# Attention units pipelined in a fixed TensorE order among projection steps, and x's last transposes one block later

## The chip, the cores and the metric

One core of a Trainium2 chip runs the whole program in one launch. The metric is the device time of one execution in microseconds (us), median of three executions. The engines: PE (TensorE: matrix products and transposes), ACT (ScalarE), DVE (VectorE), POOL (GpSimd) and SP (which issues DMAs). Each works its own queue in the order in which its instructions were placed, and waits at an instruction until its inputs are ready and its output buffer is free.

## What is computed

Four layers of a decoder trunk, of kinds S5, HGRN2, attention, S5, on 512 tokens of width 1024. Each is `h = h + rms_norm(branch(rms_norm(h)))`. The attention layer (layer 2), cut to what matters:

```python
proj = h @ w_in                       # q 1024, k 256, v 256, z 1024
q, k = rope(q + b), rope(k + b)       # 16 query heads, 4 key heads of 64
scores = q . k / 8                    # blocks of 128 queries, this and the block before, masked
p = softmax over (scores, sink)       # the sink is one learnt logit per head
o = p @ v
out = (o * silu(z)) @ w_out
```

## The kernel before, in words

**Products.** All projections are done with three products of split numbers: hi x hi, hi x lo, lo x hi. Weights come in chunks of 256 features. ACT makes each chunk's high part (`whi`, L112), DVE its low part (`wlo`, L113). x is transposed by PE (tile `xtp`, L206), and ACT and DVE copy it out as `xh` and `xl` (L210, L211). A block of 128 features over all tokens takes 24 products `pj` 512 wide (`ws`, L146).

**Order.** A scheduler places the instructions inside each engine's queue. Its priorities follow the order in which the program is written, its choice a cost model of its own.

**First blocks of a layer** (`first_blocks`, L214): the first four blocks of features are worked in two halves of the tokens, 24 products 256 wide for each block and half. The first two blocks' first halves run first. Then the tokens' blocks 2 and 3 are transposed (`norm_xt`, L193): before the third and the fourth block's first half. In the attention layer the four blocks are k (two) and chunk 0 of q (two).

**Attention** (`layer_at`, L960). The rest of the projection is q chunks 1 to 3, v, and z chunks 0 to 3. After k and each q chunk comes `at_rope` (L875): ACT copies the products out (`rraw`, L880), four DMAs issued by ACT swap halves of the partitions (`rsw`, L884), DVE and POOL multiply by cosine and sine (L885, L886), DVE adds (L887). `rraw` and `rsw` have one buffer each.

The attention itself is `at_core(p, n)` (L889) for pair p of key heads and query block n, and each call has two units b2, so 16 units in all. A unit: four score products `scps`, two for either key head of the pair; one head lies in the upper 64 rows of PE's array, the other in the lower ("row halves"). DVE adds the mask and takes the maximum (L916), then `nm` (L920); ACT takes four exps with their sums (L925) and one more for the sink (`es`, L929); DVE adds, inverts and scales (L930, L932, L936); PE transposes the result (`ptp`, L940), ACT copies it out (`pt`, L941). After the second unit the product with v is taken (`aops`, L945) and ACT copies it over q (L949). For n = 0 scores are 128 wide, otherwise 256. A sigmoid and a multiplication for each block of z (L1013, L1014), and `at_gate` (L951) multiplies by z and splits.

PSUM banks go by tags: `ca` 2 (scores and `xtp`), `cb` 1 (`ptp`), `cc` 1 (`aops`), `pj` 4. The order in which cores, chunks of q and z, and gates are written is the table `ATSEQ` (L47): `c00 q2 c01 q3 c02 c03 z0 c10 z1 c11 ...`, and `plan_weights` (L56) loads weights in the same order.

Of the kernel before, what the change touches and what calls it, by code (L numbers as in the profile page):

```python
# [16 lines left out]
P = 128  # L17
# [28 lines left out]

ATSEQ = "c00 q2 c01 q3 c02 c03 z0 c10 z1 c11 g00 g01 z2 g02 g03 c12 z3 c13 g10 g11 g12 g13".split()  # L47


class Trunk:  # L50
# [4 lines left out]
    def plan_weights(self):  # L55
        seq = []  # L56
        for L in self.layers:
            kind, j = L % 3, L // 3
            if kind == 0:
                seq += [("s5_in", j, c) for c in range(8)]  # L60
                seq += [("s5_glu", j, c) for c in range(4)]
                o = "s5_out"
            elif kind == 1:
                for p in range(4):
                    seq += [("hg_in", j, c) for c in (p, 4 + p, 8 + p, 12 + p)]
                o = "hg_out"
            else:
                seq += [("at_in", j, c) for c in (4, 0, 5, 1) + tuple(int(t[1]) + 6 * (t[0] == "z") for t in ATSEQ if t[0] in "qz")]
# [71 lines left out]
    def ws(self, ps, w, fb, x, n0, n1):  # L140
# [73 lines left out]
    def first_blocks(self, L, evacs):  # L214
# [3 lines left out]
        for half in range(2):  # L218
            for b in range(4):
                if half == 0 and b >= 2:  # L220
                    for _ in self.norm_xt(L, (b,)):
                        pass
                self.ws(pss[b][:, half * 256:half * 256 + 256], w[b // 2], b % 2, self.x, half * 256, half * 256 + 256)
        for b in range(4):
# [664 lines left out]
    def at_core(self, p, n):  # L889

        nc, s = self.nc, self.scr
        lo = 0 if n else 128
        qs = slice(n * 128, n * 128 + 128)
        ks = slice(max(0, n - 1) * 128, n * 128 + 128)
        wd = 256 - lo
# [3 lines left out]
        ops = self.psum.tile([P, 4, 128], F32, tag="cc", name="aops", bufs=1)  # L899
        pts = [s.tile([P, 2, 4, 128], F32, tag=f"pt{i}", name="pt", bufs=1) for i in range(2)]  # L900
        f0 = lo // 128
        for b2 in range(2):
            bs = slice(2 * b2, 2 * b2 + 2)
            pss, sms = [], []
            for i in range(2):
                r = slice(64 * i, 64 * i + 64)
                ps = self.psum.tile([P, 2, 256], F32, tag="ca", name="scps", bufs=2)
                for bb in range(2):
                    nc.tensor.matmul(ps[:, bb, lo:256], lhsT=self.q[r, 4 * p + 2 * b2 + bb, qs], rhs=self.k[r, p, ks], start=True, stop=True)  # L909
                pss.append(ps)  # L910
            for i in range(2):
                sm = s.tile([P, 2, 256], F32, tag="sm", name="sm", bufs=3)
# [20 lines left out]
            for i in range(2):  # L933
                sm = sms[i]
                for bb in range(2):
                    nc.vector.tensor_scalar(out=sm[:, bb, lo:256], in0=sm[:, bb, lo:256], scalar1=rd[:, i, bb:bb + 1], scalar2=None, op0=ALU.mult)  # L936
# [4 lines left out]
                nc.scalar.activation(out=pts[i][:, f0:2, bs, :], in_=tp[:, f0:2], func=AF.Copy)  # L941
        for f in range(f0, 2):
            for i in range(2):
                kv = 2 * p + i
                nc.tensor.matmul(  # L945
                    ops[64 * i:64 * i + 64].rearrange("p b q -> p (b q)"), lhsT=self.v[:, n - 1 + f, kv * 64:kv * 64 + 64],
                    rhs=pts[i][:, f].rearrange("p b q -> p (b q)"), start=f == f0, stop=f == 1)

        nc.scalar.activation(out=self.q[:, 4 * p:4 * p + 4, qs], in_=ops, func=AF.Copy)  # L949
# [10 lines left out]
    def layer_at(self, L, nxt):  # L960
# [6 lines left out]
        with self.scratch():  # L967
# [21 lines left out]
            def qch(c):  # L989
                w = self.w_next("at_in")  # L990
                pss = []
                for fb in range(2):
                    ps = self.pj()
                    self.ws(ps, w, fb, self.x, 0, T)
                    pss.append(ps)
                self.at_rope(pss, bq[:, 2 * c:2 * c + 2], self.q[:, 2 * c:2 * c + 2, :])

            bv = s.tile([P, 2, T], F32, tag="misc", name="bv", bufs=1)[:, 0, 0:256]
# [7 lines left out]
            qch(1)  # L1006
            def zch(c):
                w = self.w_next("at_in")
                for fb in range(2):
                    ps = self.pj()  # L1010
                    self.ws(ps, w, fb, self.x, 0, T)
                    zz = self.z[:, 2 * c + fb, :]
                    nc.scalar.activation(out=zz, in_=ps, func=AF.Sigmoid)  # L1013
                    nc.vector.tensor_tensor(out=zz, in0=ps, in1=zz, op=ALU.mult)  # L1014

            for step in ATSEQ:
                if step[0] == "c":
                    self.at_core(int(step[1]), int(step[2]))
                elif step[0] == "g":
                    self.at_gate(int(step[1]), int(step[2]))  # L1020
                elif step[0] == "q":
                    qch(int(step[1]))
                else:
                    zch(int(step[1]))
# [185 lines left out]
```

## Time and profile before

| | us |
|---|---|
| median of 3 runs | 1125.99 |
| lowest, highest | 1124.99, 1126.99 |
| the profiled execution | 1127.56 |
| its span in the trace | 1125.8 |
| PE busy | 1039.3 (92%) |
| DVE busy | 783.4 (70%) |
| ACT busy | 516.8 (46%) |
| POOL busy | 233.2 (21%) |

The profiled execution is one of its own, 1.57 above the median; its span begins at the first instruction that the trace shows. The mean granted clock of PE was 0.968 of full speed. In the trace the first blocks of layers 1, 2 and 3 lie at 290 to 319, 604 to 633 and 839 to 869, the attention units, with what is left of the projection among them, at 671.5 to 806. Busy times of engines overlap, so their shares don't add up.

### The profile page before, as it was taken

To read this page: it belongs to the slowest core of one execution; us is meant where nothing else is said; L and a number is where in the kernel's file an instruction comes from. 1 tells how busy PE (TensorE), PEld (TensorE's weight loads), DVE (VectorE), ACT (ScalarE), POOL (GpSimd) and SP (SyncE) were. 2 spreads that over 40 slices of the span, in tenths; PEclk is the share of its full clock that TensorE was granted. 3 is DMA by queue.
4 is the path that set the end of the run, shared out by engine and by line. 5 is a ranking of instruction groups with operands and counts; after the bars stand their busy time and mean duration, and the time that the engine had idled before them with its cause. 6 is when DMAs were issued, how large, how long until landed. Compare 5 with 4: busy or idle time off the path is not lost.

```text
span 1125.8 us, 16828 instructions
## 1 busy us (share of the span) xinstructions
PE 1039.3 (92%) x6384; PEld 863.8 (77%) x6384; DVE 783.4 (70%) x1442; ACT 516.8 (46%) x939; POOL 233.2 (21%) x218
## 2 busy tenths in 40 slices
PE   5987898999999999999999989999998888778997
PEld 5866676878899898989888966666688676667885
DVE  6979998675566475656656455566569799995752
ACT  5444444754332324142344344888545254446540
POOL 2165553210200000000001121100011546550200
PEclk9989989999999999999999999999999899998999
DMA  7455425333130212222123443112134644434221
GB/s 244 136 143 141 102 86 128 131 120 114 53 111 22 94 39 83 69 75 76 36 79 102 108 116 100 38 53 80 57 128 126 168 107 139 115 91 140 95 91 56
DMA packets 60320, 112.32 MB, mean 100 GB/s; under 512 B 23632, under 2 KB 33488, under 8 KB 59856
## 3 DMA queue, kind: packets, MB, share of 16 engines
q1 hardware_dynamic: 34272, 87.58, 25.5%
q10 hardware_dynamic: 25968, 23.68, 7.2%
q8 instruction: 50, 0.82, 0.3%
q14 instruction: 30, 0.25, 0.1%
HBM read 87.11 MB, written 8.39 MB: 85 GB/s over the span
## 4 chain that ended last, share of the span: by engine, by line
PE 59%; DVE 23%; issue 6%; DMA 4%; ACT 4%; POOL 3%; ACTq 1%; DVEq 0%; SPq 0%; POOLq 0%
PE pj L146 22%; PE ops L160 14%; PE zps L160 4%; DVE wlo L113 4%; PE vps L160 4%; PE sps L711 2%; PE scps L909 2%; DVE vt L483 2%; PE aops L945 2%; DVE xsw L545 2%; DMA rsw<-rraw 1%; PE ptp L940 1%; DVE vt L485 1%; DMA rotf<-rot 1%; ACT whi L112 1%
## 5 line engine op out<-in xcount | busy, mean ns | idle before, releaser
L146 PE MATMUL pj<-xh,whi 128*128 128x512 f32 (+1 forms) x656 | 238.9, 367 | 0.9 <-ACT whi L112 0.9
L146 PE MATMUL pj<-xh,wlo 128*128 128x512 f32 (+1 forms) x656 | 239.5, 366 | 0.1
L146 PE MATMUL pj<-xl,whi 128*128 128x512 f32 (+1 forms) x656 | 237.9, 364 | 1.3 <-DVE xl L211 1.3
L113 DVE TENSOR_TENSOR wlo<-wraw,whi 128x1024 fp32r<-128x1024 f32 x132 | 172.4, 1311 | 74.5 <-ACT whi L112 67.6
L112 ACT ACTIVATE whi<-wraw 128x1024 fp32r<-128x1024 f32 x132 | 138.6, 1056 | 75.8 <-PE pj L146 31.8
L146 PEld LDWEIGHTS pj<-xh,wlo 128*128 128x128 f32 x656 | 129.0, 197 | 20.6 <-issue 6.1
L146 PEld LDWEIGHTS pj<-xh,whi 128*128 128x128 f32 x656 | 128.9, 198 | 20.5 <-issue 4.8
L146 PEld LDWEIGHTS pj<-xl,whi 128*128 128x128 f32 x656 | 129.0, 197 | 18.2 <-issue 2.7
L160 PE MATMUL ops<-whi,gh 128*128 128x512 f32 x256 | 101.8, 398 | 0.3 <-ACT gh L642 0.3
L160 PE MATMUL ops<-whi,gl 128*128 128x512 f32 x256 | 100.7, 394 | 0.0
L160 PE MATMUL ops<-wlo,gh 128*128 128x512 f32 x256 | 100.3, 392 | 0.0
L160 PEld LDWEIGHTS ops<-whi,gh 128*128 128x128 f32 x256 | 48.2, 188 | 11.3 <-ACT gh L642 1.1
L160 PEld LDWEIGHTS ops<-whi,gl 128*128 128x128 f32 x256 | 48.0, 188 | 11.2 <-DVE gl L643 0.9
L160 PEld LDWEIGHTS ops<-wlo,gh 128*128 128x128 f32 x256 | 48.2, 188 | 10.8 <-issue 1.1
L484 POOL TENSOR_TENSOR t<-ap,q 128x1024 f32<-128x1024 f32 x16 | 40.3, 2519 | 74.6 <-DVE q L475 37.5
L170 POOL TENSOR_SCALAR rs_m<-po_st 128x1 f32<-128x1 f32 x16 | 3.1, 191 | 252.5 <-DVE po_st L256 252.5
L146 PE MATMUL pj<-yh,whi 128*128 128x512 f32 x128 | 49.3, 399 | 4.2 <-ACT yh L621 4.2
L170 POOL TENSOR_SCALAR rs_m<-hss 128x4 f32<-128x4 f32 x8 | 1.6, 194 | 247.9 <-DVE hss L769 247.9
L210 ACT ACTIVATE xh<-xtp,gpre 128x128 fp32r<-128x128 f32 (+1 forms) x96 | 36.2, 400 | 32.8 <-DVE xl L211 20.9
L146 PE MATMUL pj<-yl,whi 128*128 128x512 f32 x128 | 50.1, 393 | 0.0
L146 PE MATMUL pj<-yh,wlo 128*128 128x512 f32 x128 | 50.1, 392 | 0.0
L252 DVE TENSOR_TENSOR yg<-ops,gpost 128x512 f32<-128x512 f32 x32 | 22.0, 689 | 40.0 <-ACT junk L250 39.6
(266 smaller groups left out, 2293.9 us busy)
## 6 DMA issues: line engine op xcount, KB each, us to landing
wraw<-in_s_in SPq DMA_DIRECT2D x32, 512.0 KB, 4.2
wraw<-in_hg_in SPq DMA_DIRECT2D x32, 512.0 KB, 3.5
wraw<-in_at_in SPq DMA_DIRECT2D x20, 512.0 KB, 4.2
rotf<-rot SPq DMA_DIRECT2D x32, 256.0 KB, 4.4
wraw<-in_s_glu SPq DMA_DIRECT2D x16, 512.0 KB, 3.7
wraw<-in_s_out SPq DMA_DIRECT2D x16, 512.0 KB, 3.5
prm<-in_s_bc ACTq DMA_DIRECT2D x16, 256.0 KB, 2.7
ub<-ut ACTq DMA_DIRECT2D x16, 256.0 KB, 3.2
```

What stands on the lines that cost most here:

```text
L112: nc.scalar.activation(out=hi, in_=raw, func=AF.Copy)
L113: nc.vector.tensor_tensor(out=lo, in0=raw, in1=hi.bitcast(F32), op=ALU.subtract)
L146: self.nc.tensor.matmul(ps, lhsT=l[k // 4][:, k % 4, c], rhs=r[:, k, n0:n1], start=k == 0 and n == 0, stop=k == KB - 1 and n == 2)
L160: self.nc.tensor.matmul(ps, lhsT=l[:, k, c], rhs=r[k // per][:, k % per, :], start=k == 0 and n == 0, stop=k == KB - 1 and n == 2)
L210: nc.scalar.activation(out=xh[:, k, c], in_=ps[:, kk, :], func=AF.Copy, scale=g)
L252: nc.vector.tensor_tensor(out=yg[:, tb, f], in0=ps, in1=gp[:, f], op=ALU.mult)
L483: nc.vector.tensor_tensor(out=vt, in0=bc(t["ap"][:, 0, gs, 0:8].unsqueeze(3), shp), in1=bc(q[:, 0].unsqueeze(2), shp), op=ALU.mult)
L484: nc.gpsimd.tensor_tensor(out=t2, in0=bc(t["ap"][:, 1, gs, 0:8].unsqueeze(3), shp), in1=bc(q[:, 1].unsqueeze(2), shp), op=ALU.mult)
L545: nc.vector.tensor_tensor(out=xsw, in0=xsw, in1=sin, op=ALU.mult)
L711: nc.tensor.matmul(ps[:, c, :], lhsT=k[:, c * 128:c * 128 + 128], rhs=q4[:, c, :, 1, :], start=True, stop=True)
L909: nc.tensor.matmul(ps[:, bb, lo:256], lhsT=self.q[r, 4 * p + 2 * b2 + bb, qs], rhs=self.k[r, p, ks], start=True, stop=True)
L945: nc.tensor.matmul(ops[64 * i:64 * i + 64].rearrange("p b q -> p (b q)"), lhsT=self.v[:, n - 1 + f, kv * 64:kv * 64 + 64], rhs=pts[i][:, f ...
```

## The change

`at_core` is cut into three parts, `scores(b2)`, `probs(b2)` and `outputs()`. PE's order in the stage is no longer the scheduler's: inside `manual_schedule` PE's instructions stand as they are written, while ACT's, DVE's and POOL's are still placed by the scheduler. A generator `rest()` gives q chunks 2 and 3 and z chunks 0 to 3 in steps of three products, 96 steps in all, and `pump(n)` takes n of them. The scores' products alternate between the row halves. Outside of this, q chunk 1 is written before v, the gates come as soon as their two z chunks are done, the weights are loaded in the order k, q0, q1, v, q2, q3, z0 to z3, and `sm` has four buffers in place of three. In `first_blocks`, for all four layers, the transposes of token block 2 stand before the fourth block's first half, and those of block 3 after all first halves.

```diff
-                if half == 0 and b >= 2:
-                    for _ in self.norm_xt(L, (b,)):
+                if half == 0 and b == 3:
+                    for _ in self.norm_xt(L, (2,)):
                         pass
                 self.ws(pss[b][:, half * 256:half * 256 + 256], w[b // 2], b % 2, self.x, half * 256, half * 256 + 256)
+            if half == 0:
+                for _ in self.norm_xt(L, (3,)):
+                    pass
...
+        def scores(b2):
+            pss = [self.psum.tile([P, 2, 256], F32, tag="ca", name="scps", bufs=2) for _ in range(2)]
+            for bb in range(2):
+                for i in range(2):
+                    r = slice(64 * i, 64 * i + 64)
+                    nc.tensor.matmul(pss[i][:, bb, lo:256], lhsT=self.q[r, 4 * p + 2 * b2 + bb, qs], rhs=self.k[r, p, ks], start=True, stop=True)
...
-                sm = s.tile([P, 2, 256], F32, tag="sm", name="sm", bufs=3)
+                sm = s.tile([P, 2, 256], F32, tag="sm", name="sm", bufs=4)
...
+        def probs(b2):
+            for i, sm in enumerate(held.pop(b2)):
                 tp = self.psum.tile([P, 2, 2, 128], F32, tag="cb", name="ptp", bufs=1)
                 for bb in range(2):
                     for f in range(f0, 2):
                         nc.tensor.transpose(tp[:, f, bb, :], sm[:, bb, f * 128:f * 128 + 128], self.ident)
+                nc.scalar.activation(out=held["pts"][i][:, f0:2, bs, :], in_=tp[:, f0:2], func=AF.Copy)
+                yield
...
+            def rest():
+                for c in (2, 3):
+                    yield from qch(c)
+                for c in range(4):
+                    yield from zch(c)
+                    zs[0] = c + 1
...
+            def pump(n):
+                for _ in range(n):
+                    next(more, None)
+                for p in range(2):
+                    while ready[p] and zs[0] >= 2 * p + 2:
+                        self.at_gate(p, ready[p].pop(0))
+            with self.tc.manual_schedule(engines={mybir.EngineType.PE}):
+                pump(8)
+                cores = {}
+                units = [(p, n, b2) for p in range(2) for n in range(4) for b2 in range(2)]
+                for u in range(len(units) + 1):
+                    if u < len(units):
+                        p, n, b2 = units[u]
+                        if b2 == 0:
+                            cores[p, n] = self.at_core(p, n)
+                        cores[p, n][0](b2)
+                        pump(3)
+                    else:
+                        pump(96)
+                    if u:
+                        p, n, b2 = units[u - 1]
+                        for _ in cores[p, n][1](b2):
+                            pump(1)
+                        if b2 == 1:
+                            cores.pop((p, n))[2]()
+                            ready[p].append(n)
+                pump(1)
```

In the rows below a line number is that of the kernel they belong to, so the same operation has another one after the change. PE in the middle of the stage, before: the first half's transposes of one unit, the second's, and the second two scores of a later unit (its first two, tile 6582, stand 27 rows ahead), with projection products between.

```order
L940 MATMUL ptp_6518<-cst_72,sm_6499 128x128 x4
L146 MATMUL pj_6704<-xh_5459,wlo_6419 128x512
L146 MATMUL pj_6704<-xh_5459,whi_6418 128x512
L146 MATMUL pj_6704<-xl_5460,whi_6418 128x512
L146 MATMUL pj_6704<-xh_5459,wlo_6419 128x512
L940 MATMUL ptp_6526<-cst_72,sm_6502 128x128 x4
L146 MATMUL pj_6704<-xh_5459,whi_6418 128x512
L909 MATMUL scps_6585<-k_5669,q_5660 128x256 x2
```

And PE in a unit after the change, the row halves' tiles 6385 and 6386 first; nine projection products follow the scores (the last is shown), then the unit before's transposes.

```order
L913 MATMUL scps_6385<-k_5669,q_5660 128x256
L913 MATMUL scps_6386<-k_5669,q_5660 128x256
L913 MATMUL scps_6385<-k_5669,q_5660 128x256
L913 MATMUL scps_6386<-k_5669,q_5660 128x256
...
L147 MATMUL pj_6357<-xh_5459,wlo_6180 128x512
L950 MATMUL ptp_6423<-cst_72,sm_6313 128x128 x4
L147 MATMUL pj_6429<-xh_5459,whi_6175 128x512
L147 MATMUL pj_6429<-xl_5460,whi_6175 128x512
L147 MATMUL pj_6429<-xh_5459,wlo_6176 128x512
L950 MATMUL ptp_6433<-cst_72,sm_6316 128x128 x4
```

Before, the second pair of a unit's scores stands apart from the first; after, the four stand together, and a fixed number of products stands before and between the transposes.

ACT in the units of the first z blocks, before: exps (L925), es, the copies `pt` (L941), the sigmoid with table loads (L1013).

```order
L925 ACTIVATE sm,dn<-sm,nm 128x256 x4
L929 ACTIVATE es<-es 128x4
L1013 ACT_TABLE_LOAD
L1013 ACTIVATE z<-pj 128x512
L112 ACTIVATE whi<-wraw 128x1024
L941 ACTIVATE pt<-ptp 128x2x256 x2
L925 ACT_TABLE_LOAD
L925 ACTIVATE sm,dn<-sm,nm 128x256 x4
L929 ACTIVATE es<-es 128x4
```

The same after (exps L929, es L933, copies L951, sigmoid L1021, output copy L964).

```order
L929 ACTIVATE sm,dn<-sm,nm 128x256 x4
L933 ACTIVATE es<-es 128x4
L951 ACTIVATE pt<-ptp 128x2x256
L1021 ACT_TABLE_LOAD
L1021 ACTIVATE z<-pj 128x512
L951 ACTIVATE pt<-ptp 128x2x256
L964 ACTIVATE q<-aops 128x4x128
L929 ACT_TABLE_LOAD
L929 ACTIVATE sm,dn<-sm,nm 128x256 x4
```

After, the two copies of the unit before stand behind the exps of the unit just scored, here with a sigmoid and its table load between them.

DVE in the first blocks of layer 2, before: the angles' reduction (L324 to L331) and the low parts `xl` of the transposed blocks (L211) take turns.

```order
L324 TENSOR_SCALAR red_n<-at_th 128x512
L325 TENSOR_SCALAR red_n<-red_n 128x512
L327 SCALAR_TENSOR_TENSOR at_th<-red_n,at_th 128x512
L211 SCALAR_TENSOR_TENSOR xl<-xtp,gpre,xh 128x128
L327 SCALAR_TENSOR_TENSOR at_th<-red_n,at_th 128x512
L211 SCALAR_TENSOR_TENSOR xl<-xtp,gpre,xh 128x128 x2
```

And after, with the same operations at L329 to L336 and L213.

```order
L329 TENSOR_SCALAR red_n<-at_th 128x512
L330 TENSOR_SCALAR red_n<-red_n 128x512
L332 SCALAR_TENSOR_TENSOR at_th<-red_n,at_th 128x512 x3
L333 TENSOR_SCALAR at_th<-at_th 128x512
L335 TENSOR_SCALAR red_n<-at_th 128x512
L336 TENSOR_TENSOR red_n<-red_n,at_th 128x512
L877 TENSOR_SCALAR sincos<-sincos,cst 128x512
L213 SCALAR_TENSOR_TENSOR xl<-xtp,gpre,xh 128x128 x16
```

After, all of the angles' work stands ahead of all sixteen copies.

## Rows read from the trace of the kernel before

In the timelines a row gives start and duration in us, engine, line, operation, output<-inputs, shape and how many records it takes together; in brackets the idle time before it and what ended that.

**Rows 1.** The page: busy time, share of the span and number of instructions of each engine; then the chain of work that ended last, share of the span by engine.
```profile
PE 1039.3 (92%) x6384; PEld 863.8 (77%) x6384; DVE 783.4 (70%) x1442; ACT 516.8 (46%) x939; POOL 233.2 (21%) x218
...
PE 59%; DVE 23%; issue 6%; DMA 4%; ACT 4%; POOL 3%; ACTq 1%; DVEq 0%; SPq 0%; POOLq 0%
```

**Rows 2.** Busy times by window, the attention units: window, its length, busy us (and instructions) of each engine, granted clock of PE, share of the DMA engines, GB/s.
```profile
671.50:806.00 134.50, 134.35 (x583) 88.39 (x584) 80.67 (x287) 98.00 (x228) 6.83 (x2) 0.99 0.20 63
```

**Rows 3.** The same view for one tile alone: the score tiles in two windows, and the output tile `aops`; the first busy time is PE's.
```profile
640.00:671.50 31.50, 0.72 (x8) 0.53 (x8) 0.91 (x4) 1.00 0.43 117
671.50:806.00 134.50, 29.57 (x120) 17.73 (x120) 21.95 (x60) 0.99 0.20 63
...
671.50:806.00 134.50, 20.51 (x56) 5.12 (x56) 4.37 (x8) 0.99 0.20 63
```

**Rows 4.** Timeline of PE, three places in the stage.
```profile
671.55 1.23 PE L909 MATMUL scps<-k,q 64*128 64x128 f32 x8 [3.75 <-DVE q L887]
...
684.11 1.13 PE L909 MATMUL scps<-k,q 64*128 64x256 f32 x4
685.17 1.07 PE L945 MATMUL aops<-pt,av 128*64 128x512 f32 x2
...
721.10 0.40 PE L146 MATMUL pj<-xl,whi 128*128 128x512 f32 x1
721.33 0.60 PE L940 MATMUL ptp<-cst,sm 128*128 128x128 f32 x4
721.86 2.69 PE L945 MATMUL aops<-pt,av 128*64 128x512 f32 x8
724.48 1.13 PE L909 MATMUL scps<-k,q 64*128 64x256 f32 x8
```

**Rows 5.** Timeline of ACT in a unit of the stage.
```profile
731.28 0.58 ACT L941 ACTIVATE pt<-ptp 128x512 f32<-128x512 f32 x1
731.75 0.50 ACT L925 ACTIVATE sm<-sm,nm 128x256 f32<-128x256 f32 x1
...
732.25 0.49 ACT L925 ACTIVATE sm<-sm,nm 128x256 f32<-128x256 f32 x1
...
733.23 0.19 ACT L929 ACTIVATE es<-es 128x4 f32<-128x4 f32 x1
...
734.39 1.28 ACT L1013 ACT_TABLE_LOAD   x1
735.88 0.60 ACT L1013 ACTIVATE z<-pj 128x512 f32<-128x512 f32 x1 [0.21 <-PE pj L146]
```

**Rows 6.** Timeline of DVE in a unit: two of its masks, and `nm`.
```profile
728.80 0.42 DVE L916 CUSTOM_DVE_ANT_0 sm<-scps,cst 128x256 f32<-128x256 f32 x1 [0.47 <-PE ptp L940]
...
729.15 0.42 DVE L916 CUSTOM_DVE_ANT_0 sm<-scps,cst 128x256 f32<-128x256 f32 x1
...
730.10 0.15 DVE L920 SCALAR_TENSOR_TENSOR nm<-mx,nsink 128x4 f32<-128x4 f32 x1
```

**Rows 7.** Timelines of ACT and PE around one copy of `ptp`.
```profile
746.63 0.39 ACT L941 ACTIVATE pt<-ptp 128x256 f32<-128x256 f32 x1 [1.48 <-PE ptp L940]
...
747.07 0.43 PE L940 MATMUL ptp<-cst,sm 128*128 128x128 f32 x2
```

**Rows 8.** The chain of waits ahead of 671.5, in order of time: start, us, what (the ropes of q chunks 0 and 1).
```profile
646.68 2.33 DMA rsw<-rraw
...
654.04 1.23 DVE q L887
...
658.13 0.61 ACTq L884
...
659.42 7.27 DMA rsw<-rraw
...
666.85 3.40 POOL rsw L886
```

**Rows 9.** Waits of PE by what it waited for, in the first blocks of layers 1, 2 and 3, and, last, from there to the end: us in total, times, longest.
```profile
PE xtp L206 <- DVE xl L211: 2.2, 1, 2.2
...
PE xtp L206 <- DVE xl L211: 2.5, 1, 2.5
...
PE kps L492 <- DVE vt L485: 7.3, 5, 2.4
...
PE xtp L206 <- DVE xl L211: 3.3, 1, 3.3
```

**Rows 10.** Busy times by window, columns as in rows 2: behind layer 1's wait, and at the start of the stage.
```profile
300.00:304.00 4.00, 2.02 (x13) 2.02 (x14) 2.47 (x9) 2.48 (x8) 0.39 (x1) 0.84 0.00 0
304.00:308.00 4.00, 4.00 (x27) 4.00 (x27) 1.90 (x7) 1.63 (x5) 0.00 (x0) 0.73 0.00 0
...
671.00:675.00 4.00, 3.45 (x15) 2.65 (x16) 3.08 (x12) 1.27 (x2) 0.00 (x0) 0.57 0.25 45
```

**Rows 11.** Timelines of PE and ACT in layer 1's first blocks: half-wide products, and ACT's copies of transposed slices.
```profile
299.40 0.28 PE L146 MATMUL pj<-xl,whi 128*128 128x256 f32 x1
299.52 0.28 PE L146 MATMUL pj<-xh,wlo 128*128 128x256 f32 x1
...
300.39 0.63 ACT L210 ACTIVATE xh<-xtp,gpre 128x128 fp32r<-128x128 f32 x2 [0.16 <-DVE xl L211]
301.18 0.63 ACT L210 ACTIVATE xh<-xtp,gpre 128x128 fp32r<-128x128 f32 x2 [0.16 <-DVE xl L211]
```

More of the change, by code (lines that the diff above doesn't have):

```diff
@@ L137, in w_next, with ws, ws_steps @@
         return self.wcv.pop(i)
-    def ws(self, ps, w, fb, x, n0, n1):
+    def ws(self, *args):
+        for _ in self.ws_steps(*args):
+            pass
+    def ws_steps(self, ps, w, fb, x, n0, n1):
         hi, lo = w
@@ L898, in at_core @@
         dn = s.tile([P, 2, 4], F32, tag="dn", name="dn", bufs=2)
[L899 to L902, printed above, removed]
+        held = {}
+        def scores(b2):
             bs = slice(2 * b2, 2 * b2 + 2)
-            pss, sms = [], []
-            for i in range(2):
[L906 to L911, printed above, removed]
-                sm = s.tile([P, 2, 256], F32, tag="sm", name="sm", bufs=3)
+            pss = [self.psum.tile([P, 2, 256], F32, tag="ca", name="scps", bufs=2) for _ in range(2)]
[3 more added lines that the diff above has]
+                    nc.tensor.matmul(pss[i][:, bb, lo:256], lhsT=self.q[r, 4 * p + 2 * b2 + bb, qs], rhs=self.k[r, p, ks], start=True, stop=True)
+            sms = []
+            for i in range(2):
+                sm = s.tile([P, 2, 256], F32, tag="sm", name="sm", bufs=4)
                 sms.append(sm)
@@ L933, in at_core @@
             for i in range(2):
-                sm = sms[i]
                 for bb in range(2):
-                    nc.vector.tensor_scalar(out=sm[:, bb, lo:256], in0=sm[:, bb, lo:256], scalar1=rd[:, i, bb:bb + 1], scalar2=None, op0=ALU.mult)
+                    nc.vector.tensor_scalar(out=sms[i][:, bb, lo:256], in0=sms[i][:, bb, lo:256], scalar1=rd[:, i, bb:bb + 1], scalar2=None, op0=ALU.mult)
+            held[b2] = sms
+        def probs(b2):
+            bs = slice(2 * b2, 2 * b2 + 2)
+            if b2 == 0:
+                held["pts"] = [s.tile([P, 2, 4, 128], F32, tag=f"pt{i}", name="pt", bufs=1) for i in range(2)]
+            for i, sm in enumerate(held.pop(b2)):
                 tp = self.psum.tile([P, 2, 2, 128], F32, tag="cb", name="ptp", bufs=1)
@@ L940, in at_core, with outputs @@
                         nc.tensor.transpose(tp[:, f, bb, :], sm[:, bb, f * 128:f * 128 + 128], self.ident)
[L941 to L949, printed above, removed]
+                nc.scalar.activation(out=held["pts"][i][:, f0:2, bs, :], in_=tp[:, f0:2], func=AF.Copy)
+                yield
+        def outputs():
+            pts = held.pop("pts")
+            ops = self.psum.tile([P, 4, 128], F32, tag="cc", name="aops", bufs=1)
+            for f in range(f0, 2):
+                for i in range(2):
+                    kv = 2 * p + i
+                    nc.tensor.matmul(
+                        ops[64 * i:64 * i + 64].rearrange("p b q -> p (b q)"), lhsT=self.v[:, n - 1 + f, kv * 64:kv * 64 + 64],
+                        rhs=pts[i][:, f].rearrange("p b q -> p (b q)"), start=f == f0, stop=f == 1)
+            nc.scalar.activation(out=self.q[:, 4 * p:4 * p + 4, qs], in_=ops, func=AF.Copy)
+        return scores, probs, outputs
     def at_gate(self, p, n):
@@ L993, in qch, with zch @@
                     ps = self.pj()
-                    self.ws(ps, w, fb, self.x, 0, T)
+                    yield from self.ws_steps(ps, w, fb, self.x, 0, T)
                     pss.append(ps)
                 self.at_rope(pss, bq[:, 2 * c:2 * c + 2], self.q[:, 2 * c:2 * c + 2, :])
+            def zch(c):
+                w = self.w_next("at_in")
+                for fb in range(2):
+                    ps = self.pj()
+                    yield from self.ws_steps(ps, w, fb, self.x, 0, T)
+                    zz = self.z[:, 2 * c + fb, :]
+                    nc.scalar.activation(out=zz, in_=ps, func=AF.Sigmoid)
+                    nc.vector.tensor_tensor(out=zz, in0=ps, in1=zz, op=ALU.mult)
+            for _ in qch(1):
+                pass
             bv = s.tile([P, 2, T], F32, tag="misc", name="bv", bufs=1)[:, 0, 0:256]
@@ L1016, in layer_at @@
[L1016 to L1024, printed above, removed]
+            zs = [0]
+            ready = {0: [], 1: []}
+            def rest():
[4 more added lines that the diff above has]
+                    zs[0] = c + 1
```

17 lines of the change are left out of this document (5 added, 12 removed).

## The prediction

> **What bounds the kernel now.** I read the page first: TensorE is busy for 92% of the span and is the largest part of the chain that ended last [rows 1]. A share over four layers says little about the one stage that is rewritten, so the windows come next: between 671.5 and 806.0, where the attention units run, PE is busy for 134.35 of 134.50 us at a granted clock of 0.99, while DVE works 80.67 and ACT 98.00 us [rows 2]. The reader is to see that PE never starves there. Whatever shortens PE's own work is a gain, and whatever makes PE wait is a full loss. The timeline shows what PE's work costs, the ACT and DVE timelines how fast they could feed a stricter order.
>
> **1. The scores side by side: -13.9 us.** All score products together keep PE busy for 0.72 + 29.57 = 30.29 us [rows 3]. A product leaves two records. Two products of one row half, 256 wide, take 1.06 us from start to the next start (684.11 to 685.17). Where all four of a unit stand next to each other they take less than their sum: 0.72 for the eight records of the only unit that ran before 671.5, 128 wide [rows 3]; and the group at 724.48 has 256-wide products of one half next to 128-wide ones of the other, eight records in the 1.13 that four of one half take alone [rows 4]. So the halves run together where they are neighbours, and in most units of the kernel before they aren't. After: 12 units of 1.13 and four of 0.72, 16.4 us. That is -13.9. Its bounds are 0 (two full-width halves don't overlap; no row shows two) and -15, with 1.06 for a unit.
>
> **2. Output products no longer cut: -1.0 us.** A full group takes 2.62 us (721.86 to 724.48) [rows 4], a group of the first query block half as much: six and two make 18.3 against 20.51 busy now [rows 3]. Busy times overstate by some tenths per group; I take -1.0 (0 to -2). Copies, exps, masks and transposes keep their number; two or three table loads fewer fall on ACT, which costs nothing off PE's path.
>
> **3. The regular stall: +9.8 us.** PE's order is now a list, so PE stands still wherever its next item isn't ready. Walk one unit from the first score at t = 0. Scores end at 1.06; nine projection products at 0.23 with 0.1 to restart bring the first transposes to 3.27, three more products let the second half's transposes be wanted at 4.46 [rows 4]. They need the one bank of tag cb, so ACT must have copied the first half out. In ACT's order that copy stands behind four exps and the small es exp of the unit just scored, in 13 of 15 units. DVE: four masks at 0.35 from 1.18 on, nm behind them at about 2.7 [rows 6]. ACT: four exps at 0.49 to 4.71, es 0.1, the copy 0.58 to 5.39 [rows 5]. PE starts when a copy ends: the copy at 746.63 lasts until 747.02, the next transposes start at 747.07 [rows 7]. So the second transposes start at 5.45, not 4.46: 1.0 us in each of the eight plain units, 0.9 in two that differ a little, +9.8 together. The units of the first query block, with half the width, lose about 0.1. Bounds: 0 if the copy comes first, 16 if all units pay.
>
> **4. The gates of z: +6 us.** Eight sigmoids stand among the exps; a change of function costs a table load of 1.28 us, the sigmoid 0.60 [rows 5], so one round is 3.16 us of ACT. In three or four units it stands between the two copies of a unit or ahead of the first; twice it fits where PE is busy. I count two full rounds, 6.3, less 0.3 of cover: +6 (2 to 8). The Trainium skill (page "ScalarE: Activation LUTs", section on table sets) says to do all work of one set before switching, and gives some 2.7 us a load. The rows say 1.28; by the page's figure, an estimate, this term would be about 12.
>
> **5. Ropes of q chunks 2 and 3: +5.5 us.** They are now spread between units 1 and 5, on the same queues. Two of four DMA issues at 0.61 stand ahead of a copy (1.2), two multiplications of 1.23 ahead of unit 3's masks (2.5) [rows 8], a copy of 0.7 ahead of another, and two chances in three of a further fall of the clock at 1.7 (1.1; the price is worked out with term 7). 1.2 + 2.5 + 0.7 + 1.1 = 5.5; bounds 2 to 8.
>
> **6. The first wait: +1 us.** Before the stage PE stands 3.75 us for the rope of q chunk 1, which ends at 671.5 [rows 4]. Now chunk 1's products stand before v's, but ropes share one pair of buffers and go one after the other: chunk 0's ends at 655.27, and chunk 1's copies and DMA issues took until 659.42. Behind them come the transfer, 3.40 on GpSimd and 1.23 on DVE: with chunk 0's transfer of 2.33 the end is at 666.4, with chunk 1's own of 7.27 at 671.5 [rows 8]. I take 668.7. PE has 48 products of chunk 1, 96 half-wide ones of v at 0.12 [rows 11], the 24 ahead of unit 0, unit 0's scores and nine more: 31 us from the end of the first blocks at 633.0, so it asks at 664. That is 4.7 us against 3.75. Bounds -1.5 and +4. The end of the stage, where one sigmoid, the last copies and half the gates come behind the last score, adds 0.5.
>
> **7. The transposes of x.** In each layer PE waits once for xtp: 2.2, 2.5 and 3.3 us in layers 1 to 3 [rows 9]. Behind layer 1's wait the clock falls: two windows of 4 us at 0.84 and 0.73 lose 1.7 us [rows 10]. There block 2's transposes now come 2.9 us earlier in relation to the copies they must wait for, so the 3.9 go; against it the last block's copies are no longer covered by 24 products. ACT starts a pair of slices every 0.79 us [rows 11], with DVE's pair behind it: about 1.0 before the first can be used, then eight slices at 0.40 against PE's 0.36 (three products at 0.12), 0.3, and 0.2 to restart: 1.5 back. **Layer 1: -2.4 us** (0 to -3.9). In layer 2 DVE now works its whole angle chain, and ACT the sine with its table load, ahead of the copies among which they stood before (the order shows it); an earlier start and later copies cancel, 0 (-4.2, wait and clock gone, to +2). Layer 3's wait lies ahead of kps waits on DVE of 7.3 us in five pieces [rows 9], which take back what comes early: 0. Layer 0 likewise. The S5 layers' other queues are reordered a little, 0 with ±3.
>
> **The sum.** -13.9 - 1.0 + 9.8 + 6.0 + 5.5 + 1.0 + 0.5 - 2.4 = +5.5 us. The profiled execution took 1127.56, which is 1.57 above the median of 1125.99; its durations serve for the differences, which are put on the median: **1131.5 us**. 0.2% is 2.25 us, about what a measurement of this kernel can tell from no change.
>
> **Rivals.** *PE isn't starved (faster).* The deciding point is whether the first copy of a unit ends before 4.46 us after its scores. It does if exps wait less than I walked: masks may start when the first two products are done, half a microsecond sooner, and a stall once taken gives ACT a head start. Then term 3 falls away and 4 to 6 are halved to 6.5: -14.9 + 6.5 - 2.4 = -10.8, **1115.2 us**. For it: ACT was busy for 98 of 134.5 us [rows 2], so 36 are free. Against it: ACT runs in its own order, and the walk shows the copy behind exps that can't be earlier than their scores.
>
> *Stall and gain cancel.* PE loses 18 to 22 us where I have 22.8, about **1126 us**.
>
> *The clock falls more often.* Each fall to the lower level costs 1.7 us, as the window 671 to 675 with 0.57 shows, again 4 x 0.43 [rows 10]. The falls that the rows show stand behind idle times of 2.2 us and more [rows 4, 9]; a unit with a z round or a rope in it comes near that. With five more falls: +8.5, **1140 us**. The Trainium skill (page "TensorE: Matmul & The Clock Gate", section "A second HAM failure mode: psum-queue depth-cycling") tells of a kernel whose short idles between groups of matmuls, from cycling PSUM buffers, made the clock oscillate. By that rule the one-bank stall of term 3 alone would do it. The trace can't show that yet: in the stage PE is idle for 0.15 us in all [rows 2].
>
> *The halves don't overlap.* If full-width halves queue, term 1 is 0: **1145 us**. The row at 724.48 speaks against it [rows 4].
>
> **How the numbers follow.** Forecast 0.38, cancel 0.15, PE fed 0.32, clock 0.12, no overlap 0.03. Faster by over 0.2%: 0.32, within: 0.15, slower: 0.53. The range reaches from the fed case, 1115, to just above the clock case, 1141; what lies outside is the low side of the fed case and the last rival. The forecast's own range is 1127 to 1137, from the bounds of terms 3 to 5.
>
> **What would show it.** Right: score products near 16 us busy in all; PE idle of about 1 us before every second group of ptp, released by ACT's copy; PE busy in the stage well under its length; layer 1's xtp wait gone. Wrong: ptp waiting under 0.3 us per unit (the fed case), score records that follow each other at 1.06 within a unit (no overlap), a granted clock under 0.95 in the stage (the clock case), or more than 3 us of change before the attention layer other than in layer 1's first blocks, which I set at zero.

## The result and the profile after

The changed kernel takes 1139.08 us (median of 4 runs, 1133.37 to 1140.82) against 1125.49 before: a ratio of 1.0112, 95% interval 1.0074 to 1.0151. It is slower by 13.6 us; 5.5 were forecast, and the range reached to 1141. The profiled execution, the slowest of the four, took 1140.82 with a span of 1139.0, against 1127.56 and 1125.8; the two are compared below. All differences by stage are between single traces; every ratio compares with runs of the kernel before on the same chip.

The page of the changed kernel, as in [rows 1]: engines, then the chain that ended last.

```profile
PE 1024.6 (90%) x6384; PEld 851.1 (75%) x6384; DVE 794.0 (70%) x1442; ACT 512.9 (45%) x937; POOL 234.6 (21%) x218
...
PE 54%; DVE 26%; ACT 8%; issue 5%; DMA 4%; POOL 3%; ACTq 1%; DVEq 0%; POOLq 0%; SPq 0%
```

PE is busy for 14.7 us less and the program is 13.2 us longer: less work, and more waiting. ACT's share of the chain doubles. Where the time lies shows when both traces are cut at the same events, the first product of each layer. Layer 0 is 3.0 us longer (290.1 to 293.1), layer 1 is 3.5 shorter, the attention layer 16.7 longer (234.9 to 251.6), layer 3 with the end 2.9 shorter. The attention layer's window, before and after (columns as in [rows 2]):

```profile
604.10:839.00 234.90, 228.55 (x1146) 171.66 (x1145) 138.74 (x377) 139.93 (x306) 21.59 (x20) 0.99 0.27 83
```

```profile
603.50:855.10 251.60, 221.80 (x1145) 166.10 (x1145) 143.89 (x376) 134.73 (x303) 20.34 (x20) 0.95 0.26 77
```

PE's idle time went from 6.4 to 29.8 us, and the granted clock from 0.99 to 0.95. PE's waits in that window, after:

```profile
PE ptp L950 <- ACT pt L951: 19.3, 13, 3.7
PE scps L913 <- DVE q L892: 6.0, 1, 6.0
PE xtp L208 <- DVE xl L213: 3.4, 1, 3.4
PE ptp L950 <- DVE sm L939: 0.9, 2, 0.6
```

Thirteen waits for a copy out of the one bank `cb` make 19.3 us where there were none before. The one wait for the rope grew from 3.75 to 5.96. One unit shows how a wait comes about: the timelines of PE, DVE and ACT from its first score at 716.42.

```profile
716.42 1.14 PE L913 MATMUL scps<-k,q 64*128 64x256 f32 x8
...
719.70 0.60 PE L950 MATMUL ptp<-cst,sm 128*128 128x128 f32 x4
...
722.00 0.66 PE L950 MATMUL ptp<-cst,sm 128*128 128x128 f32 x4 [1.00 <-ACT pt L951]
...
719.09 0.17 DVE L924 SCALAR_TENSOR_TENSOR nm<-mx,nsink 128x4 f32<-128x4 f32 x1
...
719.29 0.51 ACT L929 ACTIVATE sm<-sm,nm 128x256 f32<-128x256 f32 x1 [1.52 <-DVE nm L924]
...
721.27 0.19 ACT L933 ACTIVATE es<-es 128x4 f32<-128x4 f32 x1
721.37 0.57 ACT L951 ACTIVATE pt<-ptp 128x512 f32<-128x512 f32 x1
```

The rows are not all of the unit's: of the four exps only the first is shown. The first transposes are done at about 720.1, but their copy starts at 721.37, behind `nm`, four exps and es; the second transposes begin 5.58 us after the first score. The prediction's walk had 5.45 and a stall of 1.0; the trace says 1.00. The score row above also shows the gain: eight records in 1.14 us. All scores of the stage are busy for

```profile
640.00:813.00 173.00, 18.65 (x128) 11.78 (x128) 21.50 (x64) 0.93 0.24 71
```

18.65 us instead of 30.29 [rows 3], some of it at the low clock.

A second gain was not in the forecast's picture. The output products `aops` of a pair of heads, which write to either half of the columns, also run side by side where both inputs are there. The first group below takes 1.99 us, where the prediction has 2.62 for a full group; in the second one half's products run alone until the other half's copy has ended, at 724.34, and it takes 3.04:

```profile
707.07 1.99 PE L960 MATMUL aops<-pt,av 128*64 128x512 f32 x8
723.28 3.04 PE L960 MATMUL aops<-pt,av 128*64 128x512 f32 x8
...
723.75 0.59 ACT L951 ACTIVATE pt<-ptp 128x512 f32<-128x512 f32 x1
```

The low clock is the part that I had too small. The four longest waits of the stage:

```profile
670.80 1.23 PE L913 MATMUL scps<-k,q 64*128 64x128 f32 x8 [5.96 <-DVE q L892]
683.59 0.44 PE L950 MATMUL ptp<-cst,sm 128*128 128x128 f32 x2 [1.93 <-ACT pt L951]
695.48 1.11 PE L950 MATMUL ptp<-cst,sm 128*128 128x128 f32 x4 [3.66 <-ACT pt L951]
740.37 1.11 PE L950 MATMUL ptp<-cst,sm 128*128 128x128 f32 x4 [3.13 <-ACT pt L951]
```

Four stretches of the stage ran at half level (1.2 of 2.4 GHz), the first four windows here. The last two windows are others, with waits of 1.63 and 1.60 us, and of 1.00 and 1.03, and no fall:

```profile
667.50:674.30 6.80, 3.50 (x14) 2.79 (x15) 3.61 (x17) 1.76 (x6) 1.99 (x1) 0.51 0.00 0
684.60:688.00 3.40, 3.40 (x11) 1.49 (x12) 1.48 (x2) 0.60 (x1) 1.51 (x1) 0.51 0.04 11
694.70:701.50 6.80, 6.02 (x19) 4.17 (x20) 3.03 (x15) 1.89 (x6) 0.00 (x0) 0.51 0.00 0
739.20:746.00 6.80, 5.63 (x15) 2.35 (x15) 0.73 (x2) 1.70 (x4) 0.00 (x0) 0.50 0.17 65
703.00:720.00 17.00, 13.77 (x74) 9.07 (x72) 9.45 (x35) 9.49 (x29) 0.52 (x1) 1.00 0.33 94
720.00:735.00 15.00, 12.94 (x65) 7.76 (x64) 11.43 (x35) 10.28 (x25) 1.85 (x1) 1.00 0.01 1
```

Each stretch begins in one of the four longest waits or, the second, 1.0 us behind it. With the fall in the first blocks, half level lasts 27.3 us in the attention layer, against 6.8 before. PE was busy in 22.4 and 6.4 of these and lost half: 11.2 and 3.2 us. So the layer's +16.7 is PE's own work -14.7 (225.3 to 210.6, its busy time less the loss), idle time +23.4 and the clock +8.0.

### The profile page after: what moved, and what is told of

Read it like the earlier page. It is cut to its first block, busy times and chain, and to the rows that moved or that the text cites. A ratio compares the mean times of both kernels' runs of the same rounds, so it can differ in the third digit from the quotient of the medians.

```text
span 1139.0 us, 16826 instructions
## 1 busy us (share of the span) xinstructions
PE 1024.6 (90%) x6384; PEld 851.1 (75%) x6384; DVE 794.0 (70%) x1442; ACT 512.9 (45%) x937; POOL 234.6 (21%) x218
## 4 chain that ended last, share of the span: by engine, by line
PE 54%; DVE 26%; ACT 8%; issue 5%; DMA 4%; POOL 3%; ACTq 1%; DVEq 0%; POOLq 0%; SPq 0%
PE pj L147 19%; PE ops L162 13%; DVE wlo L109 4%; PE zps L162 4%; PE vps L162 4%; PE sps L716 2%; DVE vt L488 2%; ACT sm L929 2%; DVE vt L490 1%; ACT whi L108 1%; DVE xsw L550 1%; PE aops L960 1%; DVE sg L645 1%; DVE xa L551 1%; DMA rsw<-rraw 1%
## 5 line engine op out<-in xcount | busy, mean ns | idle before, releaser
L147 PE MATMUL pj<-xl,whi 128*128 128x512 f32 (+1 forms) x656 | 234.6, 360 | 2.5 <-DVE xl L213 2.5
L147 PE MATMUL pj<-xh,wlo 128*128 128x512 f32 (+1 forms) x656 | 233.9, 358 | 0.1
L147 PEld LDWEIGHTS pj<-xl,whi 128*128 128x128 f32 x656 | 127.8, 195 | 16.7 <-DVE xl L213 2.8
L520 POOL TENSOR_TENSOR t2w<-ap,prm 128x1024 f32<-128x1024 f32 x16 | 39.8, 2488 | 51.5 <-DVE vt L490 51.5
```

The source lines that it names most:

```text
L520: nc.gpsimd.tensor_tensor(out=t2, in0=bc(t["ap"][:, 1, gs, 1:9].unsqueeze(3), shp), in1=bc(s2.unsqueeze(2), shp), op=ALU.mult)
```

## The experiments

**Which part does what?** The first blocks alone, in the kernel before:

```diff
-                if half == 0 and b >= 2:
-                    for _ in self.norm_xt(L, (b,)):
+                if half == 0 and b == 3:
+                    for _ in self.norm_xt(L, (2,)):
...
+            if half == 0:
+                for _ in self.norm_xt(L, (3,)):
+                    pass
```

> The kernel before with the transposes of x one block later and nothing else. Theory (the stages add): the traces show layer 0 +3.0 us, layer 1 -3.5, layer 3 -2.9 for the whole change, outside the attention layer; if these come from the first blocks, this kernel is at 1125.5 - 3.4 = 1122, with the xtp wait of layer 1 gone and no fall of the clock behind it. Rival: what moved in layers 0 and 3 is a reshuffle that comes with the attention's program (other weights' order, other priorities): then only layer 1 moves, and layers 0 and 3 stay within 1 us of before.

It took 1120.54 us, a ratio of 0.9950 (0.9931 to 0.9970). This half of the change is a gain by itself. Layer 1's first blocks (its start to v's) take 25.2 us against 28.7. They take the same in the changed kernel, where that window has no wait of PE and a full clock:

```profile
293.10:318.30 25.20, 25.18 (x210) 24.81 (x209) 15.26 (x30) 13.02 (x28) 4.34 (x9) 1.00 0.20 64
```

Layer 3 is 4.8 us shorter, layer 0 and the attention layer 2.1 and 1.7 longer: neither the theory's +3.0 and -2.9 nor the rival's 0. The other half is the changed kernel with the old order of x's transposes (the diff above, reversed):

> The changed kernel with x's transposes where they stood before. Theory (the stages add): 1139.1 + 3.4 = 1142, layer 2 as long as in the changed kernel within 2 us, PE's waits for ACT's copies near 20 us in all. Rival: the attention order loses because of what the first blocks hand over (a late rope): then layer 2 is shorter than in the changed kernel by more than 3 us and the time under 1138.

It took 1137.12 us, a ratio of 1.0097 (1.0071 to 1.0122). The waits for copies are there (20.8 us), so the attention order loses by itself. The ratios of the halves, 0.9950 and 1.0097, make 1.005 together, and the whole change 1.0112: some 7 us, give or take 6, come only where both are in. By its numbers the rival came true (the layer is 247.4 us, 4.2 shorter), but not by its cause: the wait for the rope is 6.6 us, no shorter. What differs is the clock, at half level for 13.7 us of the layer against 27.3; whether the hand-over or chance decides that stays open. Nor do the stages add up: layer 3 is 4.7 us shorter here as well, with x's old order. For what belongs to one execution, the kernel before ran once more:

> The kernel before once more, for its stages: in the profiles of all kernels tried so far layer 0's first blocks are some 2 us longer and layer 3 some 3 to 7 us shorter than in the one profile of before, the attention kernel with x's old order too. If that is the spread of one execution: layer 3 near 275 us here too. If it belongs to the changes: layer 3 at 279, layer 0's first kps at 57.

The one run took 1128.41 us. Layer 3, with the end, took 286.3 us, and 286.8 in the first profile (278.9 and 279.3 counted from x's last scaling, as in the expectation). In the twelve traces of kernels that were changed it takes 279.2 to 284.1, so its shortening goes with the changes, in either half. Layer 0's kps began at 58.5 against 57.0 (59.7 in the changed kernel), so about half of layer 0's loss is the spread. In layer 3 PE's idle and its own work agree within 1 us between before and after, and the clock gives 3.3 us back, more than the 2.9; why it falls less there stays open.

**Is it the one bank?** The second half's transposes go to the output product's bank, which is free by then:

```diff
-                tp = self.psum.tile([P, 2, 2, 128], F32, tag="cb", name="ptp", bufs=1)
+                tp = self.psum.tile([P, 2, 2, 128], F32, tag=("cb", "cc")[i], name="ptp", bufs=1)
```

> The changed kernel, with the second half's transposes in the bank of the output product (tag cc) and so not waiting for the first half's copy. Theory (one bank between two halves, copy behind the exps): PE's waits of ptp for ACT's copy fall from 19.3 to under 8 us, some of it comes back as waits of aops for the second copy (about 0.3 us in each second unit), falls of the clock in the stage from four to two or fewer: 1127 to 1131. Rival (ACT has too much to do in a unit, whatever the bank): the wait moves to aops and the next transposes, and the time stays at 1137 to 1140.

It took 1125.58 us, a ratio of 1.0005 (0.9988 to 1.0021): 13 us of the loss are gone, and no wait of ptp for a copy is left. PE's waits in its attention layer, and the layer's window:

```profile
PE aops L960 <- ACT pt L951: 11.5, 6, 5.3
PE scps L913 <- DVE q L892: 6.8, 1, 6.8
PE xtp L208 <- DVE xl L213: 3.4, 1, 3.4
PE ptp L950 <- DVE sm L939: 2.5, 2, 2.0
```

```profile
601.80:841.80 240.00, 214.53 (x1146) 164.59 (x1145) 141.21 (x377) 134.32 (x303) 22.37 (x20) 0.95 0.28 81
```

The time shows that the one bank costs the 13 us, but the way is not the one that I had said. More of the waits came back at aops (11.5, not some 2), so that PE's idle time in the layer fell by 4.3 only (29.8 to 25.5). The clock stayed at half level in four stretches of the stage, not two, and cost 2.3 less. The largest part, 5.1, is PE's own work: the output products, which now start when both copies are done, are busy for 16.96 us in place of 19.47, and the transposes for 18.06 in place of 19.54 (all four partly at half level). The rival is half right: the wait did move to aops, but the time did not stay.

**Is it the copy behind the exps?** The exps and all that follows are written after the copies of the unit before:

```diff
+        def softmax(b2):
+            bs = slice(2 * b2, 2 * b2 + 2)
+            sms = held[b2]
             for i in range(2):
                 for bb in range(2):
                     nc.scalar.activation(out=sms[i][:, bb, lo:256], in_=sms[i][:, bb, lo:256], func=AF.Exp, ...
...
                             cores.pop((p, n))[2]()
                             ready[p].append(n)
+                    if u < len(units):
+                        p, n, b2 = units[u]
+                        cores[p, n][3](b2)
```

> The changed kernel with each unit's exps and all behind them written after the copies of the unit before, so that ACT's order takes the copies between the exps; bank cb stays single. Theory (the copy behind four exps is what PE waits for): ptp's waits for copies fall from 19.3 to under 8 us, falls of the clock in the stage from four to two: 1126 to 1131. Rival (the exps are then late, and PE waits for the probabilities instead): waits of ptp for DVE's sm rise by over 8 us, time 1134 to 1140.

It took 1139.12 us, a ratio of 1.0112 (1.0092 to 1.0132): the rival came true. The waits changed their name and kept their sum, 29.0 us against 29.8 in the layer, and so did the half level (30.7 us).

```profile
PE ptp L954 <- DVE sm L944: 11.5, 3, 4.5
PE scps L913 <- DVE q L892: 7.2, 1, 7.2
PE ptp L954 <- ACT pt L955: 6.8, 9, 2.1
```

**Is it the sigmoids' table loads?** The gate is written with tanh, which may share the exps' table:

```diff
-        nc.vector.tensor_tensor(out=og, in0=self.q[d], in1=self.z[d], op=ALU.mult)
+        nc.vector.scalar_tensor_tensor(out=og, in0=self.q[d], scalar=0.5, in1=self.z[d], op0=ALU.mult, op1=ALU.mult)
...
-                    nc.scalar.activation(out=zz, in_=ps, func=AF.Sigmoid)
-                    nc.vector.tensor_tensor(out=zz, in0=ps, in1=zz, op=ALU.mult)
+                    nc.scalar.activation(out=zz, in_=ps, func=AF.Tanh, scale=0.5)
+                    nc.vector.scalar_tensor_tensor(out=zz, in0=zz, scalar=1.0, in1=ps, op0=ALU.add, op1=ALU.mult)
```

> The changed kernel with z's gate as z (1 + tanh(z/2)) / 2: the sigmoid's table loads among the exps go (the trace of the exps' table shows whether tanh needs one of its own). Theory: of the 20 us of waits for copies the units with a sigmoid lose some 5, with one fall of the clock less: 1131 to 1135. Rival (table loads were hidden between units): no change within 2 us of 1139.

It took 1136.88 us, a ratio of 1.0096 (1.0068 to 1.0124), which can't be told from the changed kernel's own. Tanh needs no load of its own beside the exps: of 23 table loads in the trace 14 are gone. The waits are where they were:

```profile
PE ptp L950 <- ACT pt L951: 20.7, 13, 4.6
```

In this kernel the loads cost 2 us at most.

**Do the halves have to alternate?** The four score products in the order half 0, half 0, half 1, half 1:

> The changed kernel, with a unit's four score products in the order half 0, half 0, half 1, half 1 instead of alternating; they still stand together. If standing together is enough (as the one unit of the kernel before at 655.52 suggests): scores' busy time within 1.5 us of the 18.65 of the changed kernel, time within 3 us of 1139. If alternation is needed: a unit of 256-wide products takes about 2.1 us instead of 1.1, busy time near 30, and the time rises by up to 11 us, less what PE stands still anyway.

It took 1136.57 us, a ratio of 1.0095 (1.0067 to 1.0123), and the scores' row is

```profile
640.00:815.00 175.00, 18.16 (x128) 11.65 (x128) 21.49 (x64) 0.93 0.25 71
```

Standing together is enough: the alternation adds nothing.

**Is the first wait the serial ropes?** q chunk 1's rope in pt's two buffers, which nothing uses yet:

```diff
...
-                self.at_rope(pss, bq[:, 2 * c:2 * c + 2], self.q[:, 2 * c:2 * c + 2, :])
+                self.at_rope(pss, bq[:, 2 * c:2 * c + 2], self.q[:, 2 * c:2 * c + 2, :], ("pt0", "pt1") if c == 1 else ("rraw", "rsw"))
```

> The changed kernel with the rope of q chunk 1 in the two buffers of pt, which are not in use until unit 0's copies, so that it need not wait for chunk 0's rope. Theory (the first wait is the serial ropes): the wait of 5.96 us for q falls under 0.5 and the clock's first fall in the stage goes: 1139 - 6 - 2.5 = 1130 to 1132. Rival (the next stall only comes earlier, since ACT has the same work until unit 2): the waits for copies rise by as much, 1136 to 1140.

It took 1129.81 us, a ratio of 1.0027 (1.0014 to 1.0039), 9 us less. The wait of 5.96 and the fall of the clock in it are gone. The waits for copies hardly grew (20.0 us). The layer is 9.0 us shorter: 4.7 of it idle time, and 4.9 the clock, with half level for 13.7 us in place of 27.3; PE's own work is 0.6 more.

**What is left if all is mended?** Second bank, copies ahead, own buffers and tanh together:

> All four mends in the changed kernel: copies ahead of exps, the second half in the output product's bank, chunk 1's rope in its own buffers, the gate by tanh. Theory (idle and clock are the whole loss; PE's work at full clock is 206 to 211 us in layer 2 against 225 before): idle in layer 2 under 12 us, one or two falls of the clock, layer 2 at 222 to 228 us against 234.9 before, and with the first blocks' gain 1108 to 1116. Rival (ACT or DVE becomes the bound of the stage at about 98 of 130 us): layer 2 stays over 235 and the time at 1120 or more.

It took 1117.25 us, a ratio of 0.9917 (0.9895 to 0.9940): the changed order now beats the kernel before. It fell short of what I had said: the attention layer takes 229.3 us (222 to 228), PE's idle time in it is 18.3 and not under 12, and the time is 1.3 above the range. Two long waits are left, both for probabilities. DVE, GpSimd and PE at the second:

```profile
705.84 1.23 DVE L890 TENSOR_TENSOR rraw<-rraw,sincos 128x1024 f32<-128x1024 f32 x1 [2.08 <-ACT es L938]
706.98 2.30 DVE L939 TENSOR_TENSOR es<-dn,es 128x4 f32<-128x4 f32 x1
709.30 1.23 DVE L892 TENSOR_TENSOR q<-rraw,rsw 128x1024 f32<-128x1024 f32 x1
...
705.87 3.40 POOL L891 TENSOR_TENSOR rsw<-rsw,sincos 128x1024 f32<-128x1024 f32 x1 [25.72 <-DMA rsw<-rraw]
...
711.15 1.09 PE L954 MATMUL ptp<-cst,sm 128*128 128x128 f32 x4 [6.99 <-DVE sm L944]
```

The rope of q chunk 3, which isn't needed before unit 9, stands in DVE's queue ahead of a unit's scaling. So the DVE part of chunks 2's and 3's ropes was placed behind the scaling of units 3 and 6:

```diff
...
+                    if u in (4, 7):
+                        with self.behind(self.last_mult):
+                            turns.pop(0)()
```

> As the kernel with all four mends, and the DVE part of the ropes of q chunks 2 and 3 placed behind the scaling of units 3 and 6, when their transfers and GpSimd's part have long been done. Theory (DVE stands at the rope's sum while GpSimd still works, with the next probabilities behind it in DVE's queue): the two long waits of ptp for sm, 4.4 and 7.0 us, fall to under 1 us each, and at least one fall of the clock goes: 1117 - 10 = 1103 to 1109. Rival (DVE has too much to do there in any order): the waits stay above 5 us in all, 1113 to 1118.

It took 1105.19 us, a ratio of 0.9807 (0.9789 to 0.9826). PE's waits in the attention layer, now 221.0 us long, the layer's window, and the window of its output products:

```profile
PE ptp L961 <- DVE sm L951: 4.3, 5, 1.5
PE xtp L208 <- DVE xl L213: 3.4, 1, 3.4
PE aops L971 <- ACT pt L962: 2.4, 3, 1.7
PE scps L920 <- DVE mx L927: 1.2, 1, 1.2
```

```profile
602.10:823.10 221.00, 209.48 (x1146) 162.46 (x1145) 141.91 (x377) 117.38 (x290) 19.93 (x20) 0.98 0.30 88
...
640.00:815.00 175.00, 13.78 (x56) 3.31 (x56) 4.71 (x8) 0.99 0.31 91
```

The long waits fell as expected, though not under 1 us each (the longest is 1.5). The output products now all run side by side: 13.78 us busy, 20.51 in the kernel before [rows 3].

**Which mends does a fed stage need?** The last kernel with the sigmoid again, and with the exps written first again:

> The same with the sigmoid instead of tanh, 14 table loads more at 1.28 us. If they are hidden wherever PE is fed (as the tanh gate alone made 2 us at most): within 3 us of the kernel with tanh. If ACT becomes the bound in a fed stage: 5 to 10 us slower than with tanh, with waits for copies in the units with z.

With the sigmoid it took 1111.18 us, a ratio of 0.9853 (0.9837 to 0.9870): 6 us slower than with tanh. Waits for sm rise from 4.3 to 6.4, for copies at aops from 2.4 to 4.3. In the traces 3.3 us of the difference lie in the attention layer and 2.9 in layer 3, which the edit doesn't touch.

> The fastest kernel so far (1105.2, all mends with the ropes' DVE part behind), but with the exps written ahead of the unit before's copies again, as in the changed kernel. By itself that edit moved nothing (1139.1 both ways). If the second bank alone frees the copies (a wait moved from the copy to the probabilities was all that this edit did): within 3 us of 1105. If in a fed stage the copies behind four exps hold the output products back: waits of aops for copies of 0.3 us and more in the eight units that have them, and 1109 to 1114.

With the exps first it took 1108.57 us, a ratio of 0.9856 (0.9826 to 0.9886). The interval touches that of the fastest, so this is 3 to 5 us or nothing. Its waits at aops are in six groups, 6.7 us, as the second case of the expectation had it, with the ptp waits down to 1.3: again a wait that changes its name.

## Why the prediction was nearly right

**Direction and mechanism held.** The chance of slower was 0.53, and the way was the one described: a fixed PE order and one bank between two halves, with ACT's copy behind the exps. The time lies near the top of the whole range, and 2 us above the forecast's own, 1127 to 1137. That range does not follow from the bounds of terms 3 to 5, as was said: added up they reach from 1114 to 1142. In the rival in which stall and gain cancel, a loss of 18 to 22 us gives 1127 to 1131, not 1126.

**Terms 1 and 2** (-14.9): PE's own work in the attention layer fell by 14.7 at full clock. The fastest kernel shows the scores alone at 16.89 us; 16.4 was forecast. Term 2 is another matter. I had the output products as no longer cut, -1.0; in the fastest kernel, where they run side by side, they fell by 6.7. In the changed kernel late copies hold part of that back (19.47, some of it at half level), and the transposes take 19.54 in all in place of 18.50 (a group 0.66 behind a wait and 0.60 without, at 722.00 and 719.70). That the sum of terms 1 and 2 is right is thus partly luck.

**Terms 3 to 5** without the clock (20.2 and 0.5 for the end): the waits for copies and probabilities sum to 20.2. The walk of the plain unit was right to 0.1 us: four waits are 1.00 to 1.03. The ten shorter waits for copies, 0.17 to 1.63, sum to 10.5 (term 3 had 9.8), the three long ones to 8.7. How that splits between terms 4 and 5 came out otherwise. Term 4 gave the sigmoids 6 us; without table loads the waits stayed (20.7), so it was wrong by itself, and of the long waits only the one at 740.37, 3.13 us, has one in it. Two units with rope work instead had 3.66 and 1.60. Ahead of the 3.66 DVE did not only work its two multiplications, which was all that term 5 put down (2.5); between them it stood still for GpSimd's part:

```profile
686.46 1.23 DVE L890 TENSOR_TENSOR rraw<-rraw,sincos 128x1024 f32<-128x1024 f32 x1 [1.60 <-DMA rsw<-rraw]
689.94 1.23 DVE L892 TENSOR_TENSOR q<-rraw,rsw 128x1024 f32<-128x1024 f32 x1 [2.26 <-POOL rsw L891]
```

The right total is partly luck.

**Term 6** (+1): the wait was 5.96, +2.2. PE came at 664.8, as worked out; the rope ended at 670.8, near the far end of the bounds.

**Term 7**: layer 1's first blocks gave 3.5 where 2.4 was forecast. In layer 2 the wait went from 2.50 to 3.35, where I had 0. Layers 0 and 3 moved by +3.0 and -2.9, where I had 0 with ±3; about half of the +3.0 is the spread of one execution.

**The mis-sized term is the clock.** I gave it 1.1 us as part of the rope's term, and it cost 8.0 in the attention layer. The rival "the clock falls more often" (0.12, five more falls, 8.5 us) came true beside the forecast, not instead of it, and its sign too: the granted clock was 0.93 from 640 to 813, where under 0.95 was named. Its size was right, its count not: there were three falls more in the layer (five, against two), but three of them lasted 6.8 us, and two of these took about 3 us each, where every fall was priced at 1.7. Forecast and rival share their cause, and I should have added the price of falls to the long waits of terms 4 to 6 instead of holding it as a case of its own. The Trainium skill (page "TensorE: Matmul & The Clock Gate", section "A second HAM failure mode: psum-queue depth-cycling") describes this: frequent short idles of a kernel that cycles its PSUM banks bring the clock down again and again. The trace agrees in that the clock went down and up four times in the stage. But the falls go with the four longest waits, one of them for a rope, and the regular stalls of 1.00 to 1.63 us passed with the clock at 1.00. A limit can't be read from this: in the fastest kernel (1105.19) one fall stands behind a wait of 1.21, and a wait of 1.67 passed at 1.00.

**The fed rival** failed at its deciding point: the first copy ended 5.5 us after the scores, not before 4.46. It is what the mended kernels became.

## What to carry to other kernels

When the order of one engine is fixed by hand, walk one period of the engines that feed it, in the order of their queues, and look for the single buffer between two steps; that walk was right to a tenth of a microsecond in the plain units here. Add to each long wait the loss of the clock behind it: here a fall went with each of the four longest, and the clock made 8.0 of the layer's 16.7 us. And a wait often only changes its name: mend the buffer, the order and the late input together before judging a pipeline. Here single mends gave 0 to 13 us of a loss of 14, and all of them together, with the late ropes moved, turned it into a gain of 1.9%.

## What the runs showed of the hardware

Score products on the two halves of PE's rows run side by side when they are neighbours, in both orders that were tried: 1.14 us for four, 1.06 of step for two of one half. Output products on the two halves of its columns do the same when both inputs are there: eight records in 1.94 to 1.99 us, 13.78 us for all of the fastest kernel.

A DVE operation can be held by GpSimd, and the other way round. An addition of 128x4 that takes 0.16 us took 2.30 beside GpSimd's 3.40 us multiplication, and ended when that did (706.98 + 2.30 = 709.28; 705.87 + 3.40 = 709.27). The 3.40 seems to hold a wait itself: the same multiplication took 2.37 in the changed kernel where it began 0.02 us ahead of DVE's product, and the product, 1.23 elsewhere, then took 3.44:

```profile
719.48 2.37 POOL L891 TENSOR_TENSOR rsw<-rsw,sincos 128x1024 f32<-128x1024 f32 x1 [29.57 <-DVE es L932]
719.50 3.44 DVE L890 TENSOR_TENSOR rraw<-rraw,sincos 128x1024 f32<-128x1024 f32 x1
```

The Trainium skill (page "SBUF — State Buffer", section "SBUF: two separate sides") says that the two share a pair of ports which one of them holds for a whole instruction; the trace agrees for these pairs of operations.

The exps' table serves tanh: with it, 14 of 23 table loads of 1.28 us went. The sigmoid with its loads cost nothing measurable in a stage that waits elsewhere, and 6 us in one that is fed, of which the traces place 3.3 in that stage's layer.
